# A hybrid encoder layer on one core: the per-layer embedding product is formed beside the fourth attention head, and the last gate reads x before its norm

## The chip, the cores and the metric

The kernel runs on one core of a Trainium2 chip. The core has five engines that run their own instruction lists in order: TensorE (PE in the profile, its weight loads PEld), VectorE (DVE), ScalarE (ACT), GpSimd (POOL) and SyncE (SP, which here issues DMAs). The metric is the time of one execution on the device in microseconds (us), the median of several runs. Times of the trace are counted from the start of the span of one profiled execution.

## The reference

One layer of an encoder over 1024 tokens of width 1024, all float32:

```
h = RMSNorm(x); proj = h @ w_in
o = [ diff_attention (4 heads), bidirectional HGRN2 recurrence (4 heads) ]
x = x + o @ w_out
x = x + conv_glu(RMSNorm(x))                      # gated MLP, inner width 2816
gate = sigmoid(rmsnorm(x, norm_ple_g) @ w_ple_gate)
x = x + (p @ w_ple) * gate                        # p: (1024, 256) input embeddings
return rmsnorm(x, final_norm_g)
```

`p @ w_ple` depends on inputs alone. `rmsnorm(x, g)` is `x * rsqrt(mean(x*x) + eps) * g`, with one rsqrt per token and one `g` per column.

## The kernel before, in words

Tokens lie on the 128 partitions in 8 tiles of 128 (`NS = 8`). A matrix product is made in split precision: each operand is cut into a high and a low part (`split_into`, L145: the high part by a copy on ACT, the low part by a subtraction on DVE or POOL), and `mm3` (L153) issues three products per 128 rows of the inner dimension. Operands that lie the wrong way are turned on PE by products with an identity matrix (`transpose`).

The program is written as generators. For each head h, `attn` (L635) goes over 8 query blocks: `score` makes 12 products for two maps into two PSUM tiles "B", DVE takes the two row maxima (L665), ACT the two exps (L667), DVE joins the maps (L673); `av` turns the joined map (L685), copies it on ACT (L686) and multiplies it with v (L689). The next block's scores wait for both exps of this one. Beside the attention a `filler` yields other PE work: the projections of the recurrence's inputs of the same head (`hg_in` and `hg_in_v`: products D<-hT,w and D<-w,hT), the next head's q and k, and at the end `out_a`, half of the output projection (D<-w,osp). The recurrence `hgrn` of the head follows (L483, seven levels at L497, and so on); its F and K products are partly on POOL (L503, L509).

When the program is built, a scheduler gives each engine one fixed list, by its own estimate of durations and by the order of the code as priority. At run time an engine waits at an instruction whose inputs or buffers are not ready, and everything behind it on that engine waits too. Buffers come from pools with few slots: PSUM tiles "D" (2), "S" (2), "E" (4), SBUF weights "w" (6), raw loads "raw" (3), work tiles "c" (15).

After attention and recurrence come the second half of the output projection (`out_b`), the MLP (`up`, `down`), and the last phase, `ple` (L1290). It loads and splits `w_ple` (POOL) and `w_ple_gate` (POOL and DVE in turn, `ple_w`). For each token tile s it loads 128 rows of p, turns and splits them (`emb_T`), squares x on ACT and makes 1/rms in nine small steps on DVE (`rsq`), multiplies x by 1/rms and by the norm's weight (L202), turns the result (L1381) and splits it. `gate` then makes 48 products B<-w,h and B<-wg,h for the gate, 12 products D<-wp,pT for the embedding, the sigmoid on ACT (L1323), two DVE products with the embedding in PSUM (L1326), the sum (L1327), the final norm, and a store. The eighth tile is cut in three pieces to shorten the end.

Of the kernel before, what the change touches and what calls it, by code (L numbers as in the profile page):

```python
# [72 lines left out]
class Net:  # L73
    def __init__(self, ctx, tc, t):
# [16 lines left out]
        self.od = [pool_dram.tile([P, S], F32, name=f"od{i}") for i in range(8)]  # L91
        self.md = [pool_dram.tile([P, 8, 512], F32, name=f"md{i}") for i in range(NF // 2)]
# [152 lines left out]
    def setup2(self):  # L245
# [11 lines left out]
        nc.sync.dma_start(out=st[105:106, :], in_=t["hg_norm_g"])  # L257
        ps = self.Sm()
# [5 lines left out]
        self.norm_g = cols[:, 105:106]  # L264
        self.subln = g.tile([P, 1], F32, name="subln")
# [1002 lines left out]

    def ple_w(self):
# [3 lines left out]
        i = 0  # L1273
        for n in range(2):
            for kp in range(4):
# [10 lines left out]
                self.split_into(hi, lo, raw, nc.gpsimd if kp % 2 else nc.vector)  # L1286
                for k in range(2):
                    self.wg[n][kp * 2 + k] = (hi[:, k, :], lo[:, k, :])

    def ple(self):  # L1290
        nc, t, v = self.nc, self.t, self.nc.vector
        self.prev = self.loaded
        gb3 = self.gb_load("norm_ple_g", self.wf([1024]))
        wp = []
        for n in range(2):
            hi, lo = [self.c([2, 512], F32R, "wp") for _ in range(2)]
            raw = self.raw([2, 512])
            self.load(out=raw, in_=t["w_ple"][0][:, n * 512:n * 512 + 512].rearrange("(k p) c -> p k c", p=P))
            self.split_into(hi, lo, raw, nc.gpsimd)
            wp.append((hi, lo))  # L1300

        def gate(s, hl, pT, mid=None):
# [3 lines left out]
            psp = [self.D() for _ in range(2)]  # L1306
            sg = self.c([1024])
            xs = self.xr[s]

            def emb(tr):  # L1310
                for n in range(2):
                    with self.after(tr if n else None):
                        self.mm3(psp[n], [((pT[:, 0, k, :], pT[:, 1, k, :]), (wp[n][0][:, k, :], wp[n][1][:, k, :]))
                                          for k in range(2)])

            if not last:
                for n in range(2):
                    ns = slice(n * 512, n * 512 + 512)
                    self.mm3(psg[:, ns], [((hi[:, k, :], lo[:, k, :]), self.wg[n][k]) for k in range(8)])
                    if n == 1:  # L1320
                        tr = mid()
                emb(tr)
                nc.scalar.activation(sg, psg, AF.Sigmoid)  # L1323
                for n in range(2):
                    ns = slice(n * 512, n * 512 + 512)
                    v.tensor_tensor(out=sg[:, ns], in0=sg[:, ns], in1=psp[n], op=ALU.mult)  # L1326
# [229 lines left out]
```

## Time and profile before

| | |
|---|---|
| median of 3 runs | 1567.2 us (1566.43 to 1568.12) |
| the profiled execution | 1566.02 us, span 1564.2 us |
| mean granted TensorE clock | 0.986 |
| PE busy | 1504.1 us, 96% |
| DVE, ACT, POOL busy | 1068.6, 643.6, 553.4 us |

The span is the time from the first to the last instruction; the execution's own time is 1.8 us longer. A busy PE is not a PE at its peak: a product counts as busy until its modelled end, so products overlap in the list, and the price of one is the distance between starts. "Idle before" names what ended a wait. A granted clock of 1.00 is 2.4 GHz, 0.50 would be 1.2 GHz; a value in between is a mean over a stretch in which both occurred. The head that the change speaks of as the fourth is h = 3; its attention runs from about 558 to 641 us. The last phase runs from about 1422 us to the end.

### The profile page before, as it was taken

What the parts mean: (1) busy time and instruction counts of PE and PEld (TensorE: products, weight loads), DVE (VectorE), ACT (ScalarE), POOL (GpSimd) and SP (SyncE); (2) the same over time, 40 slices, a digit from 0 to 9 for tenths busy, and PEclk for the clock granted to TensorE, in tenths of its full rate; (3) what the DMA queues carried; (4) which work ended last, traced back from release to release, by engine and by line L of the source; (5) the groups of instructions that cost most, each with busy time, mean ns of one, the idle gap of its engine ahead of it and who ended that gap; (6) DMA issues with size and microseconds to landing.
All of it is one profiled execution on the core that took longest, in us unless ns stands there. A gap on an engine that the chain in (4) does not pass through costs nothing.

```text
span 1564.2 us, 21892 instructions
## 1 busy us (share of the span) xinstructions
PE 1504.1 (96%) x8550; PEld 1296.2 (83%) x8550; DVE 1068.6 (68%) x1612; ACT 643.6 (41%) x1068; POOL 553.4 (35%) x381
## 2 busy tenths in 40 slices
PE   8999999999999996999989999999999999999997
PEld 8969998999799985888768787887888788887886
DVE  7355575555555656757876777777777886877666
ACT  5335535642365345513544333333334233352322
POOL 3111441244104510531386666666665000064000
PEclk9999999999999999999999999999999999999999
DMA  7100011001100110133403233332235766321111
GB/s 249 41 14 15 28 55 41 28 28 42 41 15 28 54 55 27 67 109 120 159 19 95 101 102 101 102 106 97 102 127 205 253 217 217 132 58 61 35 51 41
DMA packets 99833, 134.32 MB, mean 86 GB/s; under 512 B 6048, under 2 KB 66706, under 8 KB 99730
## 3 DMA queue, kind: packets, MB, share of 16 engines
q1 hardware_dynamic: 99298, 132.07, 25.4%
q8 instruction: 67, 1.10, 0.3%
q10 hardware_dynamic: 432, 0.86, 0.1%
q14 instruction: 36, 0.29, 0.1%
HBM read 99.87 MB, written 30.93 MB: 84 GB/s over the span
## 4 chain that ended last, share of the span: by engine, by line
PE 68%; DVE 10%; issue 8%; POOL 7%; ACT 4%; DMA 2%; SPq 0%; DVEq 0%; POOLq 0%; ACTq 0%
PE D L158 31%; PE E L158 11%; PE S L158 6%; PE B L158 5%; POOL S L151 4%; PE B L497 3%; PE S L689 3%; PE B L659 3%; ACT e L667 2%; DVE atm L665 1%; PE S L685 1%; DMA raw<-in_w_ffn_gate 1%; POOL ag L1054 1%; POOL x L1235 1%; DVE cv L1028 1%
## 5 line engine op out<-in xcount | busy, mean ns | idle before, releaser
L158 PE MATMUL D<-w,hT 128*128 128x256 f32 x1920 | 256.7, 289 | 0.7 <-POOL w L151 0.3
L158 PEld LDWEIGHTS D<-w,hT 128*128 128x128 f32 x1920 | 239.0, 193 | 3.1 <-issue 1.4
L158 PE MATMUL E<-T,S 128*128 128x512 f32 x924 | 220.1, 397 | 9.2 <-DVE ag L999 5.7
L158 PEld LDWEIGHTS E<-T,S 128*128 128x128 f32 x924 | 176.0, 192 | 50.2 <-issue 4.7
L151 POOL TENSOR_TENSOR S<-w,S 128x512 fp32r<-128x512 f32 x119 | 178.7, 1519 | 104.6 <-ACT S L148 98.6
L151 POOL TENSOR_TENSOR w<-raw,w 128x1024 fp32r<-128x1024 f32 x39 | 98.8, 2537 | 276.8 <-ACT w L148 225.2
L158 PE MATMUL D<-hT,w 128*128 128x512 f32 x576 | 138.5, 396 | 0.0
L158 PEld LDWEIGHTS D<-hT,w 128*128 128x128 f32 x576 | 107.1, 189 | 24.7 <-issue 3.2
L158 PE MATMUL S<-T,S 128*128 128x512 f32 x528 | 124.2, 389 | 1.1 <-DVE T L151 1.1
L158 PE MATMUL E<-op,op 128*128 128x512 f32 x528 | 122.0, 389 | 0.0
L158 PEld LDWEIGHTS S<-T,S 128*128 128x128 f32 x528 | 99.1, 188 | 22.0 <-DVE T L151 1.5
L158 PEld LDWEIGHTS E<-op,op 128*128 128x128 f32 x528 | 99.1, 188 | 20.6
L148 ACT ACTIVATE S<-w 128x512 fp32r<-128x512 f32 x121 | 72.5, 623 | 101.4 <-PE S L158 58.2
L665 DVE TENSOR_REDUCE atm<-B 128x1 f32<-128x1024 f32 x64 | 75.3, 1219 | 44.1 <-PE B L659 44.1
L158 PE MATMUL D<-T,S 128*128 128x512 f32 x396 | 95.1, 391 | 4.1 <-ACT S L148 2.5
L158 PE MATMUL D<-w,osp 128*128 128x512 f32 x384 | 91.0, 393 | 0.0
L158 PEld LDWEIGHTS D<-T,S 128*128 128x128 f32 x396 | 73.9, 188 | 20.1 <-ACT S L148 2.7
L667 ACT ACTIVATE e<-B,atm 128x1024 f32<-128x1024 f32 x64 | 70.7, 1112 | 35.0 <-DVE atm L665 34.9
L158 PEld LDWEIGHTS D<-w,osp 128*128 128x128 f32 x384 | 71.1, 188 | 14.8 <-ACT osp L148 0.5
L151 POOL TENSOR_TENSOR S<-raw,S 128x512 fp32r<-128x512 f32 x30 | 51.2, 1707 | 84.6 <-ACT S L148 78.5
L148 ACT ACTIVATE w<-raw 128x1024 fp32r<-128x1024 f32 x44 | 46.6, 1059 | 75.9 <-PE D L158 59.4
L659 PE MATMUL B<-qkT,qkT 64*128 64x512 f32 x384 | 58.2, 426 | 15.0 <-ACT e L667 13.9
(301 smaller groups left out, 2747.5 us busy)
## 6 DMA issues: line engine op xcount, KB each, us to landing
mb<-md SPq DMA_DIRECT2D x74, 256.0 KB, 4.5
md<-ag SPq DMA_DIRECT2D x31, 512.0 KB, 3.5
raw<-in_w_in SPq DMA_DIRECT2D x40, 256.0 KB, 3.2
raw<-in_w_ffn_gate SPq DMA_DIRECT2D x20, 512.0 KB, 6.0
w<-in_w_ffn_up SPq DMA_DIRECT2D x20, 512.0 KB, 3.8
x<-in_x SPq DMA_DIRECT2D x16, 512.0 KB, 6.6
raw<-in_w_in SPq DMA_DIRECT2D x12, 512.0 KB, 4.0
w<-in_w_ffn_down SPq DMA_DIRECT2D x10, 512.0 KB, 6.7
```

The costliest lines, as they stand in the source:

```text
L148: nc.scalar.activation(hi, src, AF.Copy)
L151: (lo_eng or nc.vector).tensor_tensor(out=lo, in0=src, in1=f32(hi), op=ALU.subtract)
L158: m = self.nc.tensor.matmul(out, a, b, start=new and i == 0 and j == 0, stop=i == n - 1 and j == 2, skip_group_check=not new)
L497: nc.tensor.matmul(ps[:, c * 128:(c + 1) * 128], X[:, c * 128:(c + 1) * 128], vw(Y, [[2 * hh, 64 // hh], [1024 + hh, 2], [1, hh]], c * 128 ...
L659: mm = nc.tensor.matmul(scs[m][:, kk], qs[a][pr, qq], ks[b][pr, kk], start=j == 0, stop=j == 2).ins
L665: nc.vector.tensor_reduce(nm[:, m:m + 1], sc, AX.X, ALU.max, negate=True)
L667: self.last_exp = nc.scalar.activation(em, sc, AF.Exp, bias=nm[:, m:m + 1], accum_out=(s0 if m == 0 else s1)).ins
L685: nc.tensor.transpose(ps[:, i * 128:(i + 1) * 128], e[:, k * 128:(k + 1) * 128], self.ident)
L689: nc.tensor.matmul(po[:, 0:128], wT[:, k, :], v[:, k, :], start=(k == 0), stop=(k == 7))
L1028: v.scalar_tensor_tensor(c[:, 0:1023], a[:, 1:1024], self.cw(2, f), c[:, 0:1023], ALU.mult, ALU.add)
L1054: nc.gpsimd.tensor_tensor(out=out[k][:, h], in0=out[k][:, h], in1=g, op=ALU.mult)
L1235: self.nc.gpsimd.tensor_tensor(out=xs, in0=xs, in1=acc(i % 4), op=ALU.add)
```

## The change

The product `p @ w_ple` moves out of the last phase into a new generator `emb`, which the filler yields between the two parts of head 3's recurrence inputs. It makes all eight tiles, copies them from PSUM on ACT and stores them in DRAM (`ed`); `gate` loads each tile back. In `ple_w` the norm's weight, now a column per 128 rows of `w_ple_gate`, is multiplied into the gate's weights while they are split (ACT for the high part, a scalar_tensor_tensor on DVE for the low part). The transposes of the last phase read x itself, and 1/rms becomes the scale operand of the sigmoid. The line numbers of the changed kernel are up to 3 higher than before ahead of `emb`.

```diff
@@ setup2
+        nc.sync.dma_start(out=st[106:114, :], in_=t["norm_ple_g"].rearrange("o (k p) -> (o k) p", p=P))
...
+        self.ple_g = lambda k: cols[:, 106 + k:107 + k]
@@ new
+    def emb(self):
+        nc, t = self.nc, self.t
+        wp = []
+        for n in range(2):
+            hi, lo = self.w([2, 512]), self.w([2, 512])
+            raw = self.raw([2, 512])
+            self.load(out=raw, in_=t["w_ple"][0][:, n * 512:n * 512 + 512].rearrange("(k p) c -> p k c", p=P), free=True)
+            self.split_into(hi, lo, raw, nc.gpsimd)
+            wp.append((hi, lo))
+        yield
+        for s in range(NS):
+            pr = self.raw([256])
+            self.load(out=pr, in_=t["p"][0, 0, s * 128:(s + 1) * 128, :], free=True)
+            ps = self.D()
+            for k in range(2):
+                nc.tensor.transpose(ps[:, k * 128:(k + 1) * 128], pr[:, k * 128:(k + 1) * 128], self.ident)
+            pT = self.c([2, 2, 128], F32R, "pT")
+            self.split_into(pT[:, 0], pT[:, 1], ps[:, 0:256].rearrange("p (k s) -> p k s", k=2))
+            em = self.c([1024], name="em")
+            for n in range(2):
+                ps = self.D()
+                self.mm3(ps, [((pT[:, 0, k, :], pT[:, 1, k, :]), (wp[n][0][:, k, :], wp[n][1][:, k, :]))
+                              for k in range(2)])
+                nc.scalar.activation(em[:, n * 512:n * 512 + 512], ps, AF.Copy)
+            nc.sync.dma_start(out=self.ed[s], in_=em)
+            yield 2.9
@@ ple_w
-                self.split_into(hi, lo, raw, nc.gpsimd if kp % 2 else nc.vector)
                 for k in range(2):
+                    g = self.ple_g(kp * 2 + k)
+                    nc.scalar.activation(hi[:, k, :], raw[:, k, :], AF.Copy, scale=g)
+                    nc.vector.scalar_tensor_tensor(lo[:, k, :], raw[:, k, :], g, f32(hi[:, k, :]), ALU.mult, ALU.subtract)
@@ ple, gate
+            sg, em = self.c([1024]), self.c([1024], name="em")
+            self.load(out=em, in_=self.ed[s])
...
-                    if n == 1:
-                        tr = mid()
-                emb(tr)
-                nc.scalar.activation(sg, psg, AF.Sigmoid)
-                for n in range(2):
-                    ns = slice(n * 512, n * 512 + 512)
-                    v.tensor_tensor(out=sg[:, ns], in0=sg[:, ns], in1=psp[n], op=ALU.mult)
+                    if n == 0:
+                        mid()
+                nc.scalar.activation(sg, psg, AF.Sigmoid, scale=r)
+                v.tensor_tensor(out=sg, in0=sg, in1=em, op=ALU.mult)
@@ ple, around it
-        def norm(s):
-            return emb_T(s), self.norm_tile(self.xr[s], gb3, "n1")
...
+        def rms(s):
+            ssq, vh = self.small(1, "plq"), self.small(1, "plv")
+            nc.scalar.activation(self.c([1024], name="sq"), self.xr[s], AF.Square, accum_out=ssq)
+            v.tensor_scalar(vh, ssq, -0.5 / D, -0.5 * EPS, ALU.mult, ALU.add)
+            return self.rsq(vh, 1, "pl")
...
+        hls = [turn(0)]
...
+        for s in range(NS):
+            gate(s, hls[s], rms(s), lambda: hls.append(turn(s + 1)))
@@ build
-                    items += self.hg_in(h, st[h]) + ["hq%d" % h, self.hg_in_v(h, st[h]), "hv%d" % h]
+                    items += self.hg_in(h, st[h]) + ["hq%d" % h]
+                    if h == 3:
+                        items += [self.emb(), "emb"]
+                    items += [self.hg_in_v(h, st[h]), "hv%d" % h]
...
+                if h == 3:
+                    fill("emb")
```

On PE, in the attention of head 3, one query block stood like this before: the last score product of a block (L659), the turning of a joined map (L685), its product with v (L689), the next map's turning, and the next block's scores.

```order
L659 MATMUL B_5857<-qkT_5487,qkT_5472 128x512
L685 MATMUL S_5822<-cst,e_5756 128x128 x4
L689 MATMUL S_5828<-v_3537,wT_5815 128x128 x8
L685 MATMUL S_5882<-cst,e_5806 128x128 x4
L659 MATMUL B_5908<-qkT_5487,qkT_5471 128x512
```

In the changed kernel the same block (L662, L688 and L692 are those lines now) holds the two transposes of p (L1288) and, ahead of the next scores, the embedding's products; six more of these rows follow before the next L662.

```order
L662 MATMUL B_5800<-qkT_5496,qkT_5481 128x512
L688 MATMUL S_5781<-cst,e_5712 128x128 x4
L1288 MATMUL D_6082<-cst,raw_6080 128x128 x2
L692 MATMUL S_5787<-v_3546,wT_5774 128x128 x8
L688 MATMUL S_5825<-cst,e_5765 128x128 x4
L159 MATMUL D_6089<-w_5940,pT_6085 128x512
L159 MATMUL D_6089<-w_5941,pT_6085 128x512
L159 MATMUL D_6089<-w_5940,pT_6085 128x512 x2
L159 MATMUL D_6089<-w_5941,pT_6085 128x512
L159 MATMUL D_6089<-w_5940,pT_6085 128x512
L159 MATMUL D_6097<-w_5946,pT_6085 128x512
L159 MATMUL D_6097<-w_5947,pT_6085 128x512
```

One embedding tile so stands in each of the last five blocks of head 3 (and one in the second); two more follow behind the block's end, among the levels of the recurrence, and the products of head 3's v and gate columns, which stood in the first blocks, stand behind those.

On ACT the same block held before, between two pairs of exps (L667), the two copies of the joined map (L686) and the square and copy of its product with v (L690, L691).

```order
L667 ACTIVATE e_5806,ats_5738<-B_5791,atm_5790 128x1024
L690 ACTIVATE o_5557,atq_5558<-S_5778 128x128
L667 ACTIVATE e_5809,at_5789<-B_5792,atm_5790 128x1024
L686 ACTIVATE wT_5815<-S_5816 128x512
L691 ACTIVATE o_5557<-S_5778 128x128
L686 ACTIVATE wT_5815<-S_5822 128x512
L690 ACTIVATE o_5736,atq_5737<-S_5828 128x128
```

Now (L670 the exps, L689 the map's copies, L693 and L694 the square and copy) the two copies of an embedding tile (L1296) and the high part of the next turned p (L149) stand there.

```order
L670 ACTIVATE e_5815,ats_5747<-B_5800,atm_5799 128x1024
L670 ACTIVATE e_5818,at_5798<-B_5801,atm_5799 128x1024
L693 ACTIVATE o_5566,atq_5567<-S_5787 128x128
L689 ACTIVATE wT_5824<-S_5825 128x512
L1296 ACTIVATE em_6088<-D_6089 128x512
L694 ACTIVATE o_5566<-S_5787 128x128
L1296 ACTIVATE em_6088<-D_6097 128x512
L689 ACTIVATE wT_5824<-S_5831 128x512
L149 ACTIVATE pT_6111<-D_6108 128x256
```

The exps follow behind the last of these rows; the square no longer stands between two exps.

On PE in the last phase, between the gates of two token tiles, there stood before the end of one gate (wg), the first half of the embedding (wp), the turning of the next tile (L1381), and the second half of the embedding (its first rows shown).

```order
L158 MATMUL B_12783<-wg_12114,h_12714 128x512
L158 MATMUL D_12784<-wp_12001,pT_12643 128x512
L158 MATMUL D_12784<-wp_12002,pT_12643 128x512
L158 MATMUL D_12784<-wp_12001,pT_12643 128x512 x2
L158 MATMUL D_12784<-wp_12002,pT_12643 128x512
L158 MATMUL D_12784<-wp_12001,pT_12643 128x512
L1381 MATMUL S_12837<-cst,c_12768 128x128 x4
L1381 MATMUL S_12844<-cst,c_12768 128x128 x4
L158 MATMUL D_12785<-wp_12007,pT_12643 128x512
```

Now the turning (L1387, from x) stands in the middle of a gate, between its first (w) and its second half (wg), and nothing stands between two gates.

```order
L159 MATMUL B_12872<-w_12269,h_12800 128x512
L159 MATMUL B_12872<-w_12268,h_12801 128x512
L1387 MATMUL S_12902<-cst,x_10802 128x128 x4
L1387 MATMUL S_12909<-cst,x_10802 128x128 x4
L159 MATMUL B_12872<-wg_12276,h_12800 128x512 x2
L159 MATMUL B_12872<-wg_12276,h_12801 128x512
```

The gate thus has the next tile's operand half a gate earlier than it is used.

## Rows read from the trace of the kernel before

**Rows 1.** The page, part 1: busy time, share, instructions by engine.
```profile
PE 1504.1 (96%) x8550; PEld 1296.2 (83%) x8550; DVE 1068.6 (68%) x1612; ACT 643.6 (41%) x1068; POOL 553.4 (35%) x381
```

**Rows 2.** Timeline of PE (start, length, engine, line, tiles, [idle before <-releaser]).
```profile
631.43 2.02 PE L483 MATMUL B<-q,kd 128*128 128x128 f32 x16 [2.26 <-ACT e L667]
```

**Rows 3.** Busy time by stretch: length, five engines, granted clock, DMA share, GB/s.
```profile
567.30:578.00 10.70, 10.70 (x81) 9.75 (x80) 6.21 (x19) 6.34 (x8) 2.55 (x1) 1.00 0.13 49
578.00:587.64 9.64, 7.78 (x63) 7.01 (x62) 5.88 (x7) 6.50 (x10) 0.00 (x0) 1.00 0.14 57
587.64:596.48 8.84, 6.31 (x37) 5.05 (x38) 6.40 (x10) 6.00 (x14) 0.00 (x0) 0.81 0.36 119
...
602.90:610.87 7.97, 5.86 (x37) 4.60 (x38) 4.08 (x6) 4.08 (x12) 0.00 (x0) 0.81 0.00 0
610.87:617.56 6.69, 4.52 (x36) 3.74 (x36) 4.82 (x11) 3.81 (x10) 0.00 (x0) 1.00 0.01 2
...
sum 178.35, PE 159.55 PEld 138.31 DVE 119.23 ACT 80.00 POOL 41.23; mean PE 11.40 PEld 9.88 DVE 8.52 ACT 5.71 POOL 2.95
```

**Rows 4.** Timeline of one query block.
```profile
610.87 1.66 PE L659 MATMUL B<-qkT,qkT 64*128 64x512 f32 x12 [2.11 <-ACT e L667]
...
612.56 2.35 DVE L665 TENSOR_REDUCE atm<-B 128x1 f32<-128x1024 f32 x2
...
614.95 1.11 ACT L667 ACTIVATE e<-B,atm 128x1024 f32<-128x1024 f32 x1 [1.21 <-DVE atm L665]
...
617.56 1.67 PE L659 MATMUL B<-qkT,qkT 64*128 64x512 f32 x12 [2.17 <-ACT e L667]
```

**Rows 5.** Timeline of one token tile in the last phase.
```profile
1482.46 4.93 PE L158 MATMUL B<-w,h 128*128 128x512 f32 x21
...
1487.23 0.38 PE L1365 MATMUL S<-cst,pr 128*128 128x128 f32 x2
1487.36 0.94 PE L158 MATMUL B<-w,h 128*128 128x512 f32 x3
...
1490.72 0.34 SPq L1329 DMA_DIRECT2D out<-c  x1
...
1493.61 1.52 PE L158 MATMUL D<-wp,pT 128*128 128x512 f32 x6
1494.98 1.03 PE L1381 MATMUL S<-cst,c 128*128 128x128 f32 x8
...
1495.77 1.63 PE L158 MATMUL D<-wp,pT 128*128 128x512 f32 x6
```

**Rows 6.** Busy time by stretch, that token tile.
```profile
1482.46:1497.24 14.78, 14.78 (x72) 12.27 (x70) 9.96 (x25) 4.60 (x9) 0.00 (x0) 1.00 0.13 45
```

**Rows 7.** Groups by line in the last phase (busy, mean ns); a DMA's us to landing.
```profile
L202 DVE SCALAR_TENSOR_TENSOR c<-x,n1y,wf 128x1024 f32<-128x1024 f32 x15 | 19.3, 1284 | 0.3
...
L148 ACT ACTIVATE h<-S 128x512 fp32r<-128x512 f32 x14 | 7.6, 595 | 43.5 <-PE S L1381 43.5
...
L151 DVE TENSOR_TENSOR pT<-S,pT 128x256 fp32r<-128x256 f32 x6 | 2.5, 423 | 0.7 <-ACT pT L148 0.5
...
L148 ACT ACTIVATE pT<-S 128x256 fp32r<-128x256 f32 x6 | 2.3, 385 | 5.5 <-PE S L1365 5.5
...
x<-in_x SPq DMA_DIRECT2D x8, 512.0 KB, 4.9
```

**Rows 8.** Timeline at the entry into the last phase.
```profile
1421.62 3.39 DVE L151 TENSOR_TENSOR wg<-raw,wg 128x1024 fp32r<-128x1024 f32 x1
...
1425.67 0.69 PE L1365 MATMUL E<-cst,pr 128*128 128x128 f32 x2 [2.56 <-DVE x L1197]
```

**Rows 9.** Timeline of PE in the recurrence of head 3.
```profile
648.65 4.08 PE L158 MATMUL D<-w,hT 128*128 128x256 f32 x32
...
664.30 2.02 PE L497 MATMUL B<-Y,X 128*128 128x128 f32 x16 [1.17 <-DVE Y L507]
...
671.81 2.02 PE L497 MATMUL B<-Y,X 128*128 128x128 f32 x16 [1.61 <-DVE Y L507]
```

More of the change, by code (lines that the diff above doesn't have):

```diff
@@ L91, in __init__ @@
         self.od = [pool_dram.tile([P, S], F32, name=f"od{i}") for i in range(8)]
+        self.ed = [pool_dram.tile([P, D], F32, name=f"ed{i}") for i in range(NS)]
         self.md = [pool_dram.tile([P, 8, 512], F32, name=f"md{i}") for i in range(NF // 2)]
@@ L1272, in ple_w @@
         self.wg = [[None] * 8 for _ in range(2)]
-        i = 0
         for n in range(2):
@@ L1292, in ple, with gate @@
         self.prev = self.loaded
-        gb3 = self.gb_load("norm_ple_g", self.wf([1024]))
-        wp = []
-        for n in range(2):
[L1296 to L1302, printed above, removed]
+        def gate(s, hl, r, mid=None):
             hi, lo = hl
@@ L1305, in gate @@
             psg = None if last else self.B()
-            psp = [self.D() for _ in range(2)]
-            sg = self.c([1024])
+            sg, em = self.c([1024]), self.c([1024], name="em")
+            self.load(out=em, in_=self.ed[s])
             xs = self.xr[s]
[L1310 to L1314, printed above, removed]
             if not last:
@@ L1330, in gate @@
                 return
-            emb(None)
             q = self.small(3, "fin")
@@ L1338, in gate @@
                                             for k in range(8)])
-                nc.scalar.activation(sg[:, ns], ps[:, 0:c1 - c0], AF.Sigmoid)
-                v.tensor_tensor(out=sg[:, ns], in0=sg[:, ns], in1=psp[half][:, o], op=ALU.mult)
+                nc.scalar.activation(sg[:, ns], ps[:, 0:c1 - c0], AF.Sigmoid, scale=r)
+                v.tensor_tensor(out=sg[:, ns], in0=sg[:, ns], in1=em[:, ns], op=ALU.mult)
                 v.tensor_tensor(out=xs[:, ns], in0=xs[:, ns], in1=sg[:, ns], op=ALU.add)
@@ L1358, in ple, with turn @@
         early = [True]
[L1360 to L1391 removed]
+        def rms(s):
[3 more added lines that the diff above has]
+            return self.rsq(vh, 1, "pl")
+        def turn(s):
+            x = self.xr[s]
+            hl = hi, lo = self.c([8, 128], F32R, "h3"), self.c([8, 128], F32R, "h3")
+            for dg in range(2):
+                ps = turned()
+                for j in range(4):
+                    k = dg * 4 + j
+                    nc.tensor.transpose(ps[:, j * 128:(j + 1) * 128], x[:, k * 128:(k + 1) * 128], self.ident)
+                self.split_into(hi[:, dg * 4:dg * 4 + 4, :], lo[:, dg * 4:dg * 4 + 4, :],
+                                ps.rearrange("p (j s) -> p j s", j=4))
+            return hl
+        hls = [turn(0)]
         self.ple_w()
@@ L1395, in ple @@
         yield
-        for s in range(1, NS):
-            pT, y = nxt if s == 1 else norm(s)
-            hl = []
-            gate(*prev, turner(y, hl))
-            prev = (s, hl, pT)
-        gate(*prev)
+        for s in range(NS):
+            gate(s, hls[s], rms(s), lambda: hls.append(turn(s + 1)))
     def run(self, g):
```

28 lines of the change are left out of this document (removed).

## The prediction, made before the changed kernel was run

> **What bounds the kernel now.** I read the page's busy shares first, then the busy time by stretch, then the two places that the change touches row by row. TensorE (PE) is busy 96% of the span [rows 1]: a change pays by removing PE work or PE idle time. The change removes no PE work (the instruction lists of both kernels hold the same number of PE instructions); it moves the embedding products from the last phase, where PE is busy all 14.78 us of a token tile [rows 6], to the attention of head 3, where it idles for about a third of most blocks [rows 3]. So the question is how much of the moved work falls into gaps.
>
> What the gaps are: from 567.30 [rows 3] to 631.43, where the recurrence's first product starts [rows 2], eight query blocks of head 3 pass. In the first three, PE still has products of head 3's v and gate columns (w,hT) to fill with; in the other five it is busy about 4.5 of 6.7 us (rows 602.90 and 610.87 show two of them) [rows 3]. The wait is a ring: the 12 score products start at 610.87, DVE reduces at 612.56, ACT's two exps begin at 614.95, and the next scores start at 617.56, having waited 2.17 us for the exp [rows 4]. From 558.00 to 736.35, where the turning of the MLP's input (L872) begins and from where the order on PE is again the same in both kernels, PE idles 178.35 - 159.55 = 18.8 us [rows 3]. That is the room. Two blocks also ran at a granted clock of 0.81, part of the time at 1.2 instead of 2.4 GHz, and there PE's busy time is longer (5.86 against 4.52 us for the same work); I put that at 2.7 us for both [rows 3].
>
> **The change, part by part.** *Price of one product.* 21 products take from 1482.46 to 1487.23, 0.227 us each [rows 5]. *What the last phase loses.* A token tile takes 1497.24 - 1482.46 = 14.78 us [rows 6]. Gone per tile: 6 embedding products from 1493.61 to 1494.98 (1.37), 6 from 1495.77 to 1497.24 (1.47), two transposes of p from 1487.23 to 1487.36 (0.13) [rows 5]: 2.97 us, leaving 11.8. Times eight: 23.8 us. It counts in full only if nothing else needs more than 11.8 us per tile: DVE is busy 9.96 and ACT 4.60 now [rows 6]. From DVE goes one of two 1.28 us normalising products and the 0.42 us for p [rows 7]; the rms chain stays, the product with the embedding becomes one instruction of 1024 columns. DVE is then near 8.3 us, so the gates stay PE's. The embedding tile is loaded from DRAM (512 KB, 4.9 us to land for such a load [rows 7]) behind the store of the tile two before it; a store is issued at 1490.72 for the gate whose last product ended one tile before 1493.61, so 12 us behind it [rows 5]. The load then lands 17 us behind that gate and is wanted two gates later, after 23.6 us: covered. If it were not, 1 us late costs 1 us per tile.
>
> *Entry into the last phase.* Before the last product of the MLP PE waits 2.56 us for a bank, because DVE held a 3.39 us weight split first [rows 8]. Now DVE stands there with three half-size splits (scalar_tensor_tensor, about 0.65 us each, half of the 1.28 us of 1024 columns), without the four splits that POOL did beside it. I expect a wait of 1.4 us, a gain of 1; bounds: 2.6 gained, or 3 lost if a weight load lands late, since then the DVE queue holds up PE's bank. Sixteen scaled hi copies on ACT replace eight copies of twice the size: nothing. Last phase together: -23.8 - 1.0 = -24.8, bounds -27 and -20.
>
> *What the attention of head 3 gains.* The same 2.97 us per tile. In the five later blocks one tile stands in each, ahead of the next scores: 4.52 + 2.97 = 7.5 us of PE per block against a ring of 6.7. ACT gets per block a copy of 256 columns (0.39) and two of 512 (0.60 each) [rows 7], so 3.81 + 1.6 = 5.4 of 7.5 us; DVE 4.82 + 0.42 [rows 3, 7]. In the order the two larger copies stand behind the exps, the small one ahead of them where ACT waits for DVE anyway. So these blocks become PE's, +0.8 us each, +4.0 for five. The first three blocks lose their w,hT filler (96 of 192 products are pushed behind) and keep their ring: I work out 9, 10 and 6.8 us against 10.70, 9.64 and 8.84. The first ends earlier because the oT copies no longer wait behind products; the third because four splits of the finished heads (osp), 0.6 us of ACT each [rows 7], are moved behind it. That is -3.4, and -1.1 for five products that now stand behind the first scores. Scores to the first product of the recurrence: 4.0 - 3.4 - 1.1 = -0.5; I take -1 (bounds -6 and +8).
>
> *Behind it.* Two of eight embedding tiles (5.9) and the 96 pushed products at 4.08 / 32 = 0.126 us (12.1) [rows 9] are still to do: +18.0. They fill the waits of 1.17 and 1.61 us at 664.30 and 671.81 [rows 9], -2.8. New waits: on POOL a split of a w_in half and one of w_out stand ahead of the recurrence's F products, +1 (bounds 0 and +4). Together +16.2.
>
> *Queues.* On SP the eight 512 KB stores stand between the loads of p, and the last two ahead of loads of w_out and x; each waits for its copy on ACT, so what is behind it comes up to a block later. p is fetched three tiles ahead, and w_out and x are wanted behind the recurrence: nothing, unless that cover is gone, then up to the 4 us allowed above. One more small load in the setup, scale operands in Copy and Sigmoid: nothing.
>
> Sum: -24.8 - 1 + 16.2 = -9.6 us. Of the 23.8 us moved, about 8.6 fall into gaps, which is under half of the 18.8 of room, since most of the rest was filled with work that now runs later. Against the profiled execution (1566.0 us, span 1564.2) that gives 1556.4; the median of the runs is 1.2 us higher, 1567.2, so 1557.6. I take **1557.5**.
>
> **Weighed against the Trainium skill.** A product costs 0.227 us by the row. "TensorE: Matmul & The Clock Gate", section Back-to-back issue gap, gives 131 ns for sustained products of 512 columns. By that a tile would cost 12 x 0.131 + 0.13 = 1.7 us, the last phase would give -14.6 and the middle +9.6, where the later blocks stay with their ring: an estimate of -5 in all. The trace disagrees, and its number stands. Two blocks at 0.81 followed stretches with PE gaps of about 2 us [rows 3]. The same page, section HAM oscillation, says that gaps between bursts let the clock fall again and that work without gaps keeps it up; rival 1 takes that up.
>
> **The rivals.**
> 1. *The gaps fill completely.* The scores of the later blocks hide the embedding wholly, the clock stays at 2.4 GHz (2.7 us back), and the w,hT products fill the recurrence. For it: 18.8 + 2.7 us of room against 23.8 moved [rows 3]. Against: the first three blocks have lost their filler, and could be the ones where the clock falls now. It gives +23.8 - 21.5 = +2.3 in the middle: -22.5, about 1545; half of it 1551. By the page's rule the clock part would hold.
> 2. *The ring gets longer than PE's work: slower.* ACT and DVE run in order; if the copies of the embedding (0.39 + 1.2 us) and the DVE part (0.42) end up ahead of the reduce or the exps in each block, the ring is 6.7 + 2.0 = 8.7 us. Against: the ACT order has the large copies behind the exps, and ACT waits 1.21 us for DVE there [rows 4]. With 2.0 us more per block than I reckon without it, the five come to 8.7, 1.2 over my 7.5, and the three to 2.0 over mine: +12. PE's gaps are then as long as now in all eight, and two more blocks at the low clock cost 1.35 each: +2.7. The total is -9.6 + 14.7 = +5.1: 1572.3. It decides from 1.2 us per block over my figures in all eight (9.6 us).
> 3. *The last phase doesn't shorten as PE's work does.* DVE's in-order list or the reload sets the tile at 13.5 instead of 11.8 us: 8 x 1.7 = 13.6 lost, total +4 to no change, 1567. For it: DVE was busy 9.96 of 14.78 [rows 6], and its list now mixes two rms chains. Against: 8.3 of 11.8 leaves 3.5 us.
> 4. *Nothing is gained by moving*: all 23.8 us reappear in the middle, and only the 1 us at the entry stays: 1566.
>
> **How the numbers follow.** Forecast (-4 to -14) 0.62; rival 1 with its half (-14 and more) 0.20; rival 2 0.06; rival 3 0.06; rival 4 0.06. The middle's bounds (-6 and +8 around the blocks, 0 and +4 behind) and the last phase's make the range 1549 to 1565. About 0.2% (3.1 us) is what a measurement of this kernel can tell from no change: faster 0.87, the same 0.08 (rival 4, part of 3), slower 0.05.
>
> **What would show it.** Tile period 11.8 us between transposes in the last phase, and its last 24 us unchanged: right; over 12.5: rival 3. Blocks of head 3 of 7.3 to 7.7 us with PE busy through them: right; PE still waiting on exps at 8 us and more: rival 2. First product of head 3's recurrence (L483) near 630 us instead of 631.43: right. The turning of the MLP's input (L872) from 751 us instead of 736.35: right; 740: rival 1; 760: rivals 2 or 4. Wrong would be above all a middle that takes more than 24 us longer, or a PE wait over 5 us at the entry of the last phase.

## The result, and the profile after

Measured on one chip, the changed kernel takes 1544.03 us in the median of 4 runs (1542.62 to 1546.63), the kernel before 1567.12: a ratio of 0.9854 (0.9837 to 0.9871), 23.1 us less. Two later pairs, on other chips, gave 0.9875 (0.986 to 0.989) and 0.9859 (0.9846 to 0.9873): 19.7 and 21.3 us. The forecast was 1557.5, with a range that ended at 1549. The direction was right; the gain is more than twice the 9.6 us of the sum.

The profiled execution after took 1546.63 us. Its page, part 1, answers [rows 1]: PE does the same 8550 instructions and is busy for 97% of the span instead of 96%.

```profile
PE 1497.7 (97%) x8550; PEld 1292.2 (84%) x8550; DVE 1049.7 (68%) x1609; ACT 655.2 (42%) x1092; POOL 537.9 (35%) x377
```

Where the time went is read from busy time by stretch, cut in both kernels at the same PE instructions: the first scores of head 3, the first product of its recurrence, the turning of the MLP's input, and the end of the MLP's last run of 48 E products. First the kernel before (length, then PE, PEld, DVE, ACT, POOL, granted clock, DMA share, GB/s):

```profile
0.00:558.46 558.46, 545.35 (x3973) 500.63 (x3974) 323.60 (x602) 254.98 (x471) 167.71 (x130) 0.99 0.16 48
558.46:631.43 72.97, 57.14 (x392) 47.85 (x392) 47.98 (x93) 43.47 (x81) 5.94 (x3) 0.95 0.13 45
631.43:736.35 104.92, 101.95 (x622) 90.13 (x623) 71.25 (x126) 36.54 (x63) 35.29 (x29) 1.00 0.27 92
736.35:1421.82 685.47, 668.40 (x2934) 548.42 (x2932) 534.81 (x584) 268.00 (x381) 339.92 (x218) 0.99 0.38 129
1421.82:1564.20 142.38, 131.25 (x633) 109.21 (x631) 90.95 (x209) 40.60 (x73) 4.52 (x2) 0.97 0.12 40
```

The changed kernel, the same stretches:

```profile
0.00:556.69 556.69, 542.92 (x3974) 498.45 (x3974) 320.82 (x602) 255.25 (x471) 167.70 (x130) 0.99 0.16 48
556.69:628.06 71.37, 63.19 (x381) 50.26 (x381) 47.07 (x95) 47.20 (x92) 5.74 (x3) 0.95 0.16 61
628.06:746.57 118.51, 118.37 (x748) 106.67 (x747) 71.03 (x132) 44.40 (x78) 39.74 (x31) 1.00 0.40 131
746.57:1430.07 683.50, 667.52 (x2933) 547.99 (x2932) 538.66 (x594) 269.24 (x387) 324.74 (x214) 0.99 0.39 128
1430.07:1544.80 114.73, 105.69 (x521) 88.87 (x519) 72.11 (x189) 39.12 (x66) 0.00 (x0) 0.98 0.20 71
```

Against the forecast's terms, with a second pair of profiles (r1 and r2, one chip) beside the first:

| stretch | forecast | first pair | second pair |
|---|---|---|---|
| start to first scores | 0 | -1.8 | -3.4 |
| attention of head 3 | -1.0 | -1.6 | -1.6 |
| from the recurrence to the MLP's input | +16.2 | +13.6 | +13.9 |
| MLP | 0 | -2.0 | -1.5 |
| last phase | -24.8 | -27.7 | -27.7 |
| sum | -9.6 | -19.4 | -20.3 |

Every term erred to the same side; none erred by more than 3.4 us. The other 3.7 us of the first result (23.1 against 19.4) lie between the profiled executions and the medians.

In the attention the rows that answer [rows 2, 3] are these (PE's timeline after; in brackets the wait):

```profile
574.10 2.71 PE L662 MATMUL B<-qkT,qkT 64*128 64x512 f32 x12 [3.91 <-ACT e L670]
...
583.71 2.21 PE L662 MATMUL B<-qkT,qkT 64*128 64x512 f32 x12 [2.62 <-ACT e L670]
...
591.89 1.66 PE L662 MATMUL B<-qkT,qkT 64*128 64x512 f32 x12 [1.53 <-ACT e L670]
...
606.05 1.65 PE L662 MATMUL B<-qkT,qkT 64*128 64x512 f32 x12
...
613.41 1.65 PE L662 MATMUL B<-qkT,qkT 64*128 64x512 f32 x12
...
628.06 1.95 PE L486 MATMUL B<-q,kd 128*128 128x128 f32 x16
...
662.01 1.95 PE L500 MATMUL B<-Y,X 128*128 128x128 f32 x16
663.72 4.68 PE L159 MATMUL D<-w,hT 128*128 128x256 f32 x37
668.23 1.95 PE L500 MATMUL B<-Y,X 128*128 128x128 f32 x16
```

The five later blocks hold no wait, and four of them last 7.3 to 7.4 us: they are PE's, as forecast. The first three keep 8.1 us of waits. The last three rows answer [rows 9]: the waits of 1.17 and 1.61 us at the recurrence's levels are gone.

The last phase, one token tile (PE and SP's queue), answers [rows 5], and its stretch answers [rows 6]:

```profile
1500.83 5.61 PE L159 MATMUL B<-w,h 128*128 128x512 f32 x24
...
1506.27 1.04 PE L1387 MATMUL S<-cst,x 128*128 128x128 f32 x8
...
1507.07 5.73 PE L159 MATMUL B<-wg,h 128*128 128x512 f32 x24
...
1510.79 0.34 SPq L1344 DMA_DIRECT2D out<-c  x1
1511.22 0.38 SPq L170 DMA_DIRECT2D em<-ed  x1
1512.63 1.07 PE L159 MATMUL B<-w,h 128*128 128x512 f32 x4
```

```profile
1500.83:1512.63 11.80, 11.80 (x57) 9.84 (x56) 7.87 (x21) 4.39 (x7) 0.00 (x0) 1.00 0.26 87
```

The tile takes 11.80 us and PE is busy all of it. The reload lands in 3.7 us and no engine waits for it. The entry answers [rows 8]:

```profile
1427.47 2.06 DVE L1319 SCALAR_TENSOR_TENSOR wg<-raw,cols,wg 128x512 fp32r<-128x512 f32 x3
...
1430.07 1.30 PE L159 MATMUL D<-op,op 128*128 128x512 f32 x5
1441.89 0.84 PE L159 MATMUL B<-w,h 128*128 128x512 f32 x3
```

From 1430.07 to the first gate it takes 11.82 us instead of 17.52, without a wait.

### The profile page after: what moved, and what is told of

It is laid out like the page before. It is cut to its first block, busy times and chain, and to the rows that moved or that the text cites. A ratio compares the mean times of both kernels' runs of the same rounds, so it can differ in the third digit from the quotient of the medians.

```text
span 1544.8 us, 21985 instructions
## 1 busy us (share of the span) xinstructions
PE 1497.7 (97%) x8550; PEld 1292.2 (84%) x8550; DVE 1049.7 (68%) x1609; ACT 655.2 (42%) x1092; POOL 537.9 (35%) x377
## 4 chain that ended last, share of the span: by engine, by line
PE 63%; issue 12%; POOL 12%; DVE 6%; ACT 4%; DMA 3%; SPq 0%; POOLq 0%; ACTq 0%; DVEq 0%
PE D L159 27%; PE E L159 10%; POOL S L152 8%; PE B L159 5%; PE S L159 5%; PE S L692 4%; PE B L500 3%; PE B L662 3%; POOL ag L1057 2%; PE S L688 2%; ACT e L670 1%; POOL T L152 1%; PE B L533 1%; DMA raw<-in_w_ffn_gate 1%; DMA raw<-in_w_out 1%
## 5 line engine op out<-in xcount | busy, mean ns | idle before, releaser
L149 ACT ACTIVATE S<-w 128x512 fp32r<-128x512 f32 x121 | 73.1, 624 | 106.3 <-PE S L159 53.7
L1238 POOL TENSOR_TENSOR x<-x,acc 128x512 f32<-128x512 f32 x12 | 23.9, 2033 | 166.3 <-DVE acc L1200 166.3
L670 ACT ACTIVATE e<-B,atm 128x1024 f32<-128x1024 f32 x64 | 70.7, 1112 | 24.6 <-DVE atm L668 24.5
L149 ACT ACTIVATE w<-raw 128x1024 fp32r<-128x1024 f32 x42 | 44.5, 1062 | 76.0 <-PE D L159 51.4
```

The source lines that it names most:

```text
L149: nc.scalar.activation(hi, src, AF.Copy)
L670: self.last_exp = nc.scalar.activation(em, sc, AF.Exp, bias=nm[:, m:m + 1], accum_out=(s0 if m == 0 else s1)).ins
L1238: self.nc.gpsimd.tensor_tensor(out=xs, in0=xs, in1=acc(i % 4), op=ALU.add)
```

## Experiments

**r1, r2: both kernels again.** No edit.

> The kernel before, unchanged, for a second profiled execution. In the pair of profiles the changed kernel was ahead by 1.8 us at the first scores of head 3 (556.69 against 558.46 us) and gained 2.0 us more between the turning of the MLP's input and the end of the last long run of E products of the MLP (683.5 against 685.5 us), both in code that the change does not touch. Theory S (scatter): such differences come from one execution to the next; the second profile of the kernel before differs from the first by 1 us or more in at least one of the two stretches. Theory L (lasting): the change acts there too (one more load in the setup, other buffers); the second profile of before has 558.5 +-0.5 and 685.5 +-0.5 again.

> The changed kernel, unchanged, for a second profiled execution and more times. Theory S: first scores of head 3 anywhere between 556 and 559 us, the MLP stretch 682 to 686 us. Theory L: 556.7 +-0.5 and 683.5 +-0.5. Both theories: from the first scores to the turning of the MLP's input 189.9 us again, last phase with tiles of 11.8 us and no PE wait at its entry, within 0.5 us. Time 1542 to 1546 us.

Measured: before 1564.0 us, changed 1543.73. First scores at 559.37 and 555.95 us; MLP 682.80 and 681.32. So the MLP's stretch moves by 2 to 3 us from one execution (and chip) to the next within one kernel, which is Theory S there. The start was early again in the changed kernel, by 3.4 us; both figures lie up to 0.4 us outside the ones of Theory L, which they are nearer to. Before, at 82 us (POOL, DVE and PE, and further down the entry into the last phase):

```profile
79.29 2.39 POOL L151 TENSOR_TENSOR w<-raw,w 128x1024 fp32r<-128x1024 f32 x1
79.41 2.42 DVE L620 TENSOR_TENSOR qk<-c 128x128 f32<-128x128 f32 x1
...
81.89 1.97 PE L628 MATMUL S<-cst,qk 128*128 128x128 f32 x8 [2.62 <-DVE qk L620]
...
1418.42 3.36 POOL L151 TENSOR_TENSOR wg<-raw,wg 128x1024 fp32r<-128x1024 f32 x1
...
1419.47 3.39 DVE L151 TENSOR_TENSOR wg<-raw,wg 128x1024 fp32r<-128x1024 f32 x1
```

The changed kernel there:

```profile
81.44 0.28 DVE L623 TENSOR_TENSOR qk<-c 128x128 f32<-128x128 f32 x1
...
81.78 1.12 PE L631 MATMUL S<-cst,qk 128*128 128x128 f32 x8 [0.48 <-DVE qk L623]
...
82.30 2.36 POOL L152 TENSOR_TENSOR w<-raw,w 128x1024 fp32r<-128x1024 f32 x1 [0.92 <-ACT w L149]
```

The stretch behind it, 82 to 90 us, before and then changed:

```profile
82.00:90.00 8.00, 7.44 (x30) 5.25 (x31) 4.11 (x8) 3.67 (x5) 0.00 (x0) 0.58 0.22 66
```

```profile
82.00:90.00 8.00, 6.74 (x38) 4.77 (x37) 3.90 (x7) 3.78 (x6) 2.36 (x1) 1.00 0.22 66
```

Before, a product of q and k that takes DVE 0.28 us takes 2.42, until POOL's split ends. PE waits 2.62 us for it, and then runs at a granted clock of 0.58, most of the time at 1.2 GHz: 30 PE instructions in 8 us instead of 38. In the changed kernel that split comes behind. PE's wait is not saved, it stands earlier (in the changed kernel a wait of 2.71 us ends at 21.88, before one of 0.54 at 19.89), and the turning begins at the same time, 81.89 and 81.78 us. What is saved is the slow products: from this turning to the first scores it is 477.48 us before, 474.17 changed. Of these 3.3 us 1.7 arise up to 94 us. The other 1.6 arise at 351 us, behind a wait of 2.29 us that both kernels have, before and then changed:

```profile
351.14 3.39 PE L497 MATMUL B<-Y,X 128*128 128x128 f32 x16 [2.29 <-DVE Y L507]
```

```profile
349.34 2.02 PE L500 MATMUL B<-Y,X 128*128 128x128 f32 x16 [2.29 <-DVE Y L510]
```

That wait stands in all fifteen profiles of this case. The same 16 products behind it, with the 16 that follow, take about 1.6 us longer in seven of them (r1, r4, r5, r8, r9, r12, r13) and not in the other eight, the first pair among these. So 1.6 us of the second pair's start go with the execution and not with the change, and the change is worth 1.7 to 2.2 us there (2.2 in the first pair, where the turning begins 0.4 us later).

**r5: the start.** What moved that split, in code that the change does not touch?

```diff
-            pr = self.raw([256])
+            pr = self.raw([2, 512])[:, 0, 0:256]
```

> The changed kernel with one thing undone: the tile of p is a slice of a full-size raw buffer instead of a raw tile of 256 columns. The instruction order on PE, DVE, ACT and POOL is the same; only what loads wait for differs. In the changed kernel the fourth pair of weight loads of the setup (raw<-in_w_in at 6.4 us) is held for about 4 us, PE waits 2.5 us at 21 us instead of 2.6 us at 82 us, and from 82 us to the first scores of head 3 takes 474.2 us instead of 476.4 to 477.5. Theory B (buffers): the small tile in the raw pool changed the buffers that the setup's loads get; here the loads are issued as in the kernel before (x loads from 9.6 us), PE waits 2.6 us at 82 us again, first scores at 558.5 to 559.5 us: 2 to 3.5 us slower than the changed kernel, 1546 to 1547 us. Rival C (the extra load of the norm's weight in the setup, or chance): the same time as the changed kernel, 1543 to 1544.5 us.

PE waits 2.58 us at 81.93 again, and the first scores come at 559.72 us: Theory B, though 1.6 us of that are the slow products at 351 us, which this execution had too; 2.1 us come from the stretch behind the wait at 82 us. The other runs agree: in all nine profiles with the small tile of p PE waits 0.44 to 0.48 us at that turning, in r5 and the five profiles without the moved embedding 2.55 to 2.62 us. The small tile, which lives at 560 us, had changed which buffers the weights get from the first microseconds on, and so what each load waits for. The time, 1546.03 us, ratio 0.9875 (0.9857 to 0.9894), is too broad to show 2 to 3 us; the trace shows them.

**r9: is it the load held at 6.4 us?** On the kernel before:

```diff
...
-            raw = self.raw([4, 256])
+            raw = self.raw0 if self.pairs == 2 and kg else self.raw([4, 256])
...
```

> The kernel before with one thing added: the fourth weight tile of the setup is loaded into the buffer of the first, so its load waits for the first tile's split on POOL, as that load does in the changed kernel. Nothing else differs, the order on every engine is the same. Theory B (the setup's gain comes from that held load: PE waits 2.2 us more at 21 us, where it is hidden, and no longer 2.6 us at 82 us, with the slow products behind that wait): PE waits about 0.5 us at 82 us instead of 2.6, the first scores of head 3 start at 555 to 557.6 us instead of 558.5 to 559.4, and the kernel is 1.5 to 3.5 us faster than before. Rival C (the held load only costs): the same time as before or 1 to 3 us slower.

Rival C came: 1569.8 against 1565.37 us, ratio 1.0027 (1.0016 to 1.0038). PE waits 3.09 us at 22.11, and still 2.62 us, now at 85.67. That load alone only costs; what delays POOL's split at 79 us in the changed kernel was not shown.

**r3, r4: the two halves of the change.** r3 takes only `emb` and its reload, with `ple_w` as before; r4, on the kernel before, only `ple_g`, x as operand and `scale=r`. First r3 against the changed kernel, then r4 against the kernel before:

```diff
...
-            gate(s, hls[s], rms(s), lambda: hls.append(turn(s + 1)))
+            if 0 < s < NS - 1:
+                y = norm(s + 1)
+            gate(s, hls[s], lambda: hls.append(turn(y)))
```

```diff
...
-        turner(nxt[1], hl)()
+        turner(self.xr[0], hl)()
...
-                nc.scalar.activation(sg, psg, AF.Sigmoid)
+                nc.scalar.activation(sg, psg, AF.Sigmoid, scale=r)
...
```

> Only the embedding is moved; the gate takes the normalised x, its weights are split as before the change, without the norm's weight. Theory M (the move is the gain): tile period 11.8 to 11.9 us, middle +12 us as in the changed kernel, but the entry into the last phase keeps a PE wait of 1 to 2.5 us, since DVE still has its weight splits of 1024 columns there and the norms of the first two tiles: time 1545 to 1548 us. Theory N (the norm change makes the room on DVE): with the normalising product back on DVE, 1.28 us per tile and in the chain from x to the turned operand, the tile takes 12.5 to 13.3 us: 6 to 12 us of the gain go, 1550 to 1556 us.

> Only the norm change: the gate takes x, its weight in the gate's weights, 1/rms in the sigmoid; the embedding product stays in the last phase. Theory M: tile period 14.6 to 14.8 us as before, since PE is the bound there; only the entry gains, 1 to 2.6 us: time 1564 to 1566 us. Theory N: the tile gets shorter by 0.5 us or more without the move, 1560 us or less. If the small splits on DVE at the entry cost more than the large ones did, the entry is longer and the kernel 0 to 3 us slower than before.

r3 takes 1549.42 us (ratio 0.9909, 0.9893 to 0.9924), r4 1564.49 (1.0002, 0.9991 to 1.0013). Alone, 14.0 us and nothing; together, on the same chip, 19.7. r3's last phase takes 123.61 us where r2's takes 114.78 (r3's profile is the slowest of its four executions). Its timeline at the entry and in the last phase shows why:

```profile
1432.82 2.36 POOL L152 TENSOR_TENSOR wg<-raw,wg 128x1024 fp32r<-128x1024 f32 x1 [7.43 <-ACT wg L149]
1432.84 3.42 DVE L203 SCALAR_TENSOR_TENSOR c<-x,n1y,wf 128x1024 f32<-128x1024 f32 x1
...
1436.31 1.83 PE L1382 MATMUL E<-cst,c 128*128 128x128 f32 x8 [2.66 <-DVE c L203]
...
1502.53 1.03 PE L1382 MATMUL S<-cst,c 128*128 128x128 f32 x8
1503.82 6.01 PE L159 MATMUL B<-w,h 128*128 128x512 f32 x24 [0.25 <-ACT h L149]
...
1515.11 1.04 PE L1382 MATMUL S<-cst,c 128*128 128x128 f32 x8
```

The tile takes 12.58 us (1515.11 - 1502.53), as Theory N had it, but not for want of DVE time (DVE is busy for 9.01 of the 12.58 us): the normalised operand is late, the turning stands at the gate's end, and PE starts the next gate on an operand that is still being split, 0.8 us a tile. At the entry PE waits 2.66 us for the normalising product, 3.42 us long beside POOL. In r4 the tile is 14.73 us ((1540.96 - 1437.88) / 7): with the embedding's products there, PE is the bound and the early operand buys nothing. At r4's entry the wait behind POOL's split is gone, since nothing of the gate's weights is on POOL, but PE waits in two other places, for DVE and for the load of p:

```profile
1416.78 7.10 PE L158 MATMUL E<-op,op 128*128 128x512 f32 x30 [0.95 <-DVE x L1199]
...
1428.29 0.41 PE L1368 MATMUL E<-cst,pr 128*128 128x128 f32 x2 [1.69 <-DMA pr<-in_p]
```

Each half needs the other.

**r6: the entry.**

```diff
+                self.split_into(hi, lo, raw, nc.gpsimd if kp % 2 else nc.vector)
                 for k in range(2):
-                    g = self.ple_g(kp * 2 + k)
-                    nc.scalar.activation(hi[:, k, :], raw[:, k, :], AF.Copy, scale=g)
-                    nc.vector.scalar_tensor_tensor(lo[:, k, :], raw[:, k, :], g, f32(hi[:, k, :]), ALU.mult, ALU.subtract)
```

The kernel leaves out the multiplication by the norm's weight.

> The changed kernel with the gate's weights split as before (DVE and POOL in turn, 1024 columns each); the norm's weight is left out of the gate. It asks what took the 2.56 us wait from the entry into the last phase. My forecast's step: the wait was DVE's 3.39 us weight split, and the smaller splits shorten it; then here 1.4 to 2.6 us of waiting come back between the last long run of E products and the first gate (13.2 to 14.4 us instead of 11.8). Rival D (the wait was for the normalised operand and the turned p, which the gate no longer needs): no wait, 11.8 us, and the time of the changed kernel within 1 us.

1544.25 us (0.9859, 0.9841 to 0.9877); from the run of E products to the gate it takes 12.08 us, without a wait: the old splits do not bring the wait back, so my step falls. That is Rival D's figure, but not its reason. POOL's and DVE's rows there:

```profile
1419.45 2.44 POOL L152 TENSOR_TENSOR wg<-raw,wg 128x1024 fp32r<-128x1024 f32 x1 [0.91 <-ACT wg L149]
```

```profile
1422.89 1.21 DVE L152 TENSOR_TENSOR wg<-raw,wg 128x1024 fp32r<-128x1024 f32 x1
```

The same split takes DVE 1.21 us, since POOL is done before it begins. Before, POOL's and DVE's splits stood side by side, 3.4 us each (rows of r1 above): POOL began 1.3 us ahead of the end of the E products (1418.42 and 1419.70), here 4.1 us ahead (1419.45 and 1423.55). The two splits of `w_ple` are gone from POOL's list; the second, of 2.40 us, stood right ahead of POOL's additions, which now begin 1.8 us earlier against PE and take 22.96 us instead of 24.92. So in r6 the stall went with the moved embedding, and that x needs no norm kept r3's stall from taking its place; in r4 it went with the splits on ACT and DVE, and others took its place.

**r7, r8: where the embedding stands.** r7, and then r8, which places `emb` behind `hg_in_v(3)`:

```diff
-                if h == 3:
-                    fill("emb")
```

```diff
-                    if h == 3:
-                        items += [self.emb(), "emb"]
                     items += [self.hg_in_v(h, st[h]), "hv%d" % h]
+                    if h == 3:
+                        items += [self.emb(), "emb"]
...
-                        fill("hv%d" % h)
+                        h < 3 and fill("hv%d" % h)
```

> The changed kernel, but the filler is not told to finish the embedding ahead of head 3's recurrence: the scheduler then puts seven of the eight tiles, and all products of head 3's v and gate columns, behind the attention, where PE has no gaps. Theory G (what the move gains in the middle is PE's idle time beside the attention): the five later blocks return to their ring of 6.7 us, so the attention is some 3 to 5 us shorter, but the work behind it is 16 to 24 us longer; from the first scores to the turning of the MLP's input 201 to 208 us instead of 189.9: 11 to 18 us slower than the changed kernel. Theory H (the place does not matter much, PE would find the gaps anyhow): within 4 us of the changed kernel.

> The changed kernel with the embedding placed behind head 3's v and gate columns instead of ahead of them. The first three blocks, in which PE still waits 3.9, 2.6 and 1.5 us in the changed kernel, have w,hT products to fill with again, and fewer embedding tiles stand in the later blocks. Theory G: what counts is PE idle time up to the recurrence, and the products have no idle left to find behind it: the kernel gains what the first three waits shrink and loses what the later blocks get back; by the order one embedding tile fewer stands in the attention in all, so -4 to +4 us against the changed kernel. Theory K (clock): the two slow score groups at 574 and 583 us (2.7 and 2.2 us instead of 1.66) come from the PE waits ahead of them; with the waits filled they take 1.66 us, 2 us less.

r7: 1571.54 us, slower than before (1.0034, 1.0023 to 1.0045). Its attention and what follows:

```profile
557.58:626.44 68.86, 45.55 (x298) 36.01 (x298) 44.39 (x87) 39.94 (x74) 5.72 (x3) 0.93 0.05 15
626.44:772.72 146.28, 139.13 (x828) 120.93 (x829) 69.83 (x140) 53.40 (x96) 37.45 (x31) 1.00 0.38 128
```

The stretch takes 215.14 us, 25 more than in the changed kernel and above Theory G's 201 to 208: PE idles 23 us beside the attention and, which I had not counted, 7 us behind it, most of it at embedding products that wait 0.5 to 1.5 us for the turned p or its split. Place is worth more than the whole gain of the change. r8: 1545.17 us (0.9863, 0.9846 to 0.988), stretch 188.58, all score groups 1.66 us (Theory K); the waits of the first blocks are gone, but 7.9 us of idle time remain, 2.5 of them at the turned p or its split.

**r10 to r12: turning p one tile ahead.** r11 does it in the changed kernel, r12 in r8.

```diff
...
+        nxt = turned(0)
         for s in range(NS):
+            pT, nxt = nxt, turned(s + 1) if s < NS - 1 else None
```

> The changed kernel again, beside the three others on the same chip, as their measure: 18 to 24 us faster than the kernel before; from the first scores of head 3 to the turning of the MLP's input 189.9 us, PE waits of 3.9, 2.6 and 1.5 us in the first three blocks.

> The changed kernel with the turning of the next tile of p put ahead of this tile's products. By its order all eight embedding tiles now stand in the attention of head 3, some in the first three blocks, none behind it. Theory G (PE's idle time in the attention is what the move has to gain, 8.3 us are still left): the first three waits (3.9, 2.6 and 1.5 us) shrink, the idle time from the first scores to the turning of the MLP's input falls from 8.3 to under 5 us, and that stretch takes 184 to 187.5 us: 2.5 to 6 us faster than the changed kernel. Rival R (the ring of reduce and exps gets longer, since the copies of the embedding stand between the exps on ACT): the blocks take over 7.6 us each and nothing is gained, or 1 to 5 us are lost.

> The same turning ahead, with the embedding behind head 3's v and gate columns, which fill the first blocks. The kernel with this placement but without the turning ahead still had 7.9 us of PE idle time in the stretch, of which some 5 us were waits for the turned p or its split. Theory G: these waits go, the stretch takes 183 to 186 us instead of 189.9: 4 to 7 us faster than the changed kernel. Rival R: the waits move to the exps, 188 us or more, no gain.

On one chip: r10 1544.06, r11 1542.87 (0.9856, 0.9841 to 0.9872), r12 1537.64 us (0.9825, 0.9812 to 0.9839). r11's stretch is 186.68 us, in Theory G's range, but 6.9 us stay idle where it had under 5, one tile still stands behind the first product of the recurrence, and the times do not tell r11 from r10. r12's two stretches:

```profile
559.28:636.01 76.73, 74.40 (x532) 64.69 (x532) 49.18 (x93) 51.89 (x97) 14.05 (x6) 1.00 0.13 42
636.01:742.02 106.01, 104.28 (x596) 90.67 (x594) 72.74 (x134) 41.62 (x74) 33.41 (x28) 1.00 0.43 153
```

That is 182.74 us with 4.1 idle, against 189.9 and 8.3, and 0.3 us under Theory G's range: the fastest version, 6.4 us below the changed kernel on the same chip.

**r13: the MLP.** On the kernel before:

```diff
-        st = self.c([P])
+        st = self.raw([P])
```

> The kernel before with one tile of the setup (128 columns) taken from the pool of raw weight tiles instead of the work pool. Only the setup's small loads move a few places; everything from 100 us on has the same order on every engine, but the buffers are laid out anew, and three of the MLP's gate weight loads (raw<-in_w_ffn_gate) no longer wait for a product on PE to release their buffer, as in all kernels with the embedding moved. The forecast had the stretch from the turning of the MLP's input to the last long run of E products unchanged; it took 682.8, 685.5, 687.5 and 685.5 us in four profiles with the embedding in the last phase and 678.4 to 683.5 us in nine with it moved. Theory P (the layout of the buffers, through those loads): the PE waits for DVE of about 1.6 to 2 us at 977 and 1094 us shrink, the stretch takes 679 to 683.5 us here, and the kernel is 1.5 to 4 us faster than before. Theory Q (the moved loads and splits themselves): 683 to 687 us as before, the same time.

1567.5 against 1565.42 us (1.0015, 1.0003 to 1.0027); stretch 683.94, in Theory Q's range. Theory P falls: the layout through those three loads is not the cause. The 1.5 to 2.0 us of the MLP in the two pairs are no larger than the spread of one kernel (683.50, 681.32 and 683.12 us in three profiles of the changed kernel, 685.47 and 682.80 in two of the kernel before). Over all runs they look real: ten profiles with the moved embedding have 678.44 to 683.50 us, in the mean 681.3, and the five with the embedding in the last phase (before, r1, r4, r9, r13) 682.80 to 687.45, in the mean 685.0. What in the move does it stays open.

## Why the prediction was wrong

Of the 13.5 us between the forecast and the measured gain, 9.8 lie in the terms (first pair) and 3.7 between the profiled executions and the medians.

*Right.* The price of a product and the tile: seven tiles went from 14.60 to 11.79 us ((1541.52 - 1439.34) / 7 and (1524.41 - 1441.89) / 7). The later blocks are PE's at 7.37 us. Rivals 2, 3 and 4 did not happen: no block lengthened its ring, no reload was late, and r7, whose middle grew by 37 us (215.14 against 177.89), shows what rival 4 would have looked like, and worse.

*The attention of head 3: -1.0, measured -1.6, partly by luck.* The term of the first scores was right (-1.1). The first three blocks were to take 25.8 us and took 27.50 (564.39 to 591.89), a gain of 1.7 instead of 3.4. The five later ones were to cost 4.0 us and cost 1.2 (36.17 against 34.95): I had taken a ring of 6.7 us for blocks that took 6.99 in the mean, one of them slow, and one of the five now took only 6.79. The two errors partly cancel. The recurrence's first product came at 628.06 us, near the 630 that was named.

*Rival 1 had the time, not the reason.* It gave -22.5 from a middle of +2.3. The middle is +12.0 (189.88 - 177.89): PE's gaps did not fill completely, 8.3 us of idle time stayed and the clock fell to 0.82 and 0.79 in the second and third block, as it had in two blocks before. The time came from elsewhere.

*Entry into the last phase: -1.0, measured -3.9.* This is the step that failed most clearly: a wait that was to stay did not, and the slow products behind it were put at nothing. Of the 5.70 us that the entry lost (17.52 to 11.82), six embedding products and two transposes of p are 1.8; with the tiles' 7 x 2.81 and the tail's 2.3 (22.68 to 20.39) that is 23.8, just the forecast's other term. I let 1.4 of the 2.56 us of waiting stay and named DVE's split as its cause; r6 shows that the split was long only beside POOL's. And the wait cost more than its length. PE's rows right behind it, in the kernel before:

```profile
1426.01 3.03 PE L158 MATMUL D<-op,op 128*128 128x512 f32 x7
1428.88 2.92 PE L158 MATMUL S<-op,op 128*128 128x512 f32 x12
```

Seven products take 2.87 us from start to start, 1.3 more than seven at 0.227; in r13, where the same wait of 2.56 us left the clock at 2.4 GHz, they take 1.70 (1424.11 to 1425.81). I had priced waits by their length everywhere, and the slow clock behind them nowhere but in the attention.

*Behind the attention: +16.2, measured +13.6 to +13.9.* The moved products take 17.5 us by the rows after (96 at 0.121, and 5.9 for two tiles) where I had 18.0, with 0.126 read from a busy length instead of from start to start; the fills are 2.8 as forecast (2.97 us of idle time before, 0.14 now). The +1 for new waits on POOL did not come. About 1 us more is not accounted for.

*Start: 0, measured -1.8 and -3.4, of which 1.6 in the second pair are the execution's.* "One more small load in the setup: nothing" priced the instruction and not the layout. r5 shows that the size of p's tile is the cause; by which load it acts was not shown. I had compared the order of the setup on every engine and found it the same; the buffers, and with them what each load waits for, were not.

*MLP: 0, measured -2.0 and -1.5.* By the profiles of all runs this term was probably wrong too, by some 3 to 4 us; its cause was not found.

*Weighed against the Trainium skill.* The DVE product held up beside POOL, 2.42 us instead of 0.28, ends 0.15 us behind POOL's split. "SBUF — State Buffer", section Terms, says that DVE and GpSimd arbitrate for one pair of ports, which is held for a whole instruction while the other is fully blocked; the trace agrees, at 79 us, at 1419 us and in r3. Behind PE waits of 2.62 and 2.56 us the clock fell. "TensorE: Matmul & The Clock Gate", section HAM oscillation, says that gaps let it fall; behind the wait at 82 us it did in five of the six profiles that have it, behind the wait of 2.29 us at 351 us in seven of fifteen. In r13, whose first two groups of transposes are these, a wait of 2.55 us left it at 2.4 GHz:

```profile
82.06 1.12 PE L628 MATMUL S<-cst,qk 128*128 128x128 f32 x8 [2.55 <-DVE qk L620]
84.13 1.25 PE L628 MATMUL S<-cst,qk 128*128 128x128 f32 x8 [0.95 <-DVE qkT L151]
```

So a removed wait is worth its length where no other takes its place, as in r3 and in the setup one did, and the slow products behind it often.

## What to carry to other kernels

Work that depends on inputs alone belongs where the bounding engine idles, but its place decides: the same change gained 28 us (r12), 20 us or lost 5 us (r7), by whether its products had gaps to fill and their operand ready one step ahead. Price a removed wait of the bounding engine with the slow products behind it, and ask what runs on POOL whenever a DVE operation is several times its usual length. When a tile's size changes, look at what the loads wait for in the whole program, not at the order of instructions alone.

## Not expected of the hardware

A DVE product of 128 columns takes 0.28 us alone and 2.42 beside a POOL split of 1024 columns; a DVE split of 1024 takes 1.21 and 3.39. After one such wait of 2.62 us PE ran at a granted clock of 0.58 for 8 us. In the second and third block of the changed kernel's attention the clock is 0.82 and 0.79, behind waits of 3.91 and 2.62 us, and the 12 score products take 2.71 and 2.21 us instead of 1.66.
